# Row normalization by the sum of absolute values: moving a sixth of the scaling from ScalarE to VectorE

## The chip, the cores and the metric

The kernel runs on one core of one Trainium2 chip. The metric is device time in microseconds (us). The span of a profile is about 2 us shorter than the device time of the same run. Most executions agree within 0.3%.

The engines that matter are VectorE (DVE in the profile), ScalarE (ACT), the sequencer SP, which issues the loads, and the 16 DMA engines, which move everything between HBM (the main memory) and SBUF (the on-chip memory).

## The reference

```python
def setup_inputs():
    batch, seq, dim = 32, 512, 1024
    return {"x": np.random.randn(batch, seq, dim).astype(np.float32)}

def reference(x):
    sums = np.sum(np.abs(x), axis=-1, keepdims=True)
    return (x / (sums + 1e-8)).astype(np.float32)
```

These are 16384 rows of 1024 fp32 numbers: 67.1 MB are read and 67.1 MB written. Nothing is reused.

## The kernel before

Each of the 128 partitions gets 128 rows, 12 at a time: ten tiles of 12 rows per partition and a last one of 8. A tile is loaded, reduced, scaled in place and stored. There are four tile buffers, so up to four tiles are under way at once.

```python
    R = 12
    BUFS = 4
    # ... (piece() picks rows; pools: sbuf with BUFS buffers, stats with 4)

    def normalize(x_tile, r0, k, kv):
        s = stats.tile([P, R], FP32)
        nc.vector.tensor_reduce(out=s[:, :k], in_=x_tile[:, r0 : r0 + k, :],
            axis=mybir.AxisListType.X, op=mybir.AluOpType.add,
            apply_absolute_value=True)
        # ... add EPS to s, inv = reciprocal of s, both on VectorE
        nc.vector.tensor_mul(                       # VectorE: rows 0 .. kv-1
            out=x_tile[:, r0 : r0 + kv, :], in0=x_tile[:, r0 : r0 + kv, :],
            in1=inv[:, :kv].unsqueeze(2).to_broadcast([P, kv, d]))
        for r in range(kv, k):                      # ScalarE: rows kv .. k-1
            row = x_tile[:, r0 + r, :]
            nc.scalar.activation(out=row, in_=row,
                func=mybir.ActivationFunctionType.Copy, scale=inv[:, r : r + 1])

    with tc.manual_schedule():
        for i, k in enumerate(rows):
            x_tile = sbuf.tile([P, R, d], FP32)
            nc.sync.dma_start(out=x_tile[:, :k, :], in_=piece(x_flat, i))
            normalize(x_tile, 0, k, k // 2)
            nc.scalar.dma_start(out=piece(out_flat, i), in_=x_tile[:, :k, :])
```

A store waits for both halves of the scaling. A load waits until the store of the tile four places earlier has landed, because it needs that tile's buffer.

## Time and profile before

The median was 317.85 us (three runs, 317.69 to 318.0); the profiled run has a span of 315.8 us.

| | before |
|---|---|
| VectorE busy | 212.4 us (67%) |
| ScalarE busy | 69.0 us (22%) |
| 16 DMA engines: time of all packets | 98.9% of the span |
| traffic over the span | 425 GB/s |

From the page of the kernel before: the busy time of each engine; the DMA row of the 40 slices (tenths of busy time); the two DMA queues, q1 for loads and q10 for stores, with packets, MB and the share of 16 engines' span that the packets took.

```profile
DVE 212.4 (67%) x44; ACT 69.0 (22%) x65; POOL 0.2 (0%) x4
...
DMA  8999999999999999999999999999999999999996
...
q1 hardware_dynamic: 1584, 67.11, 49.8%
q10 hardware_dynamic: 1584, 67.11, 49.1%
```

Add the two queues: 98.9% of 315.8 us is 312.3 us in which each of the 16 engines, on average, was moving a packet. So at most 3.5 us can be gained without making the traffic itself cheaper.

The window table of the same kernel agrees. Its columns are the stretch, its length, the busy time of each engine with its instructions, the clock, the DMA share, and GB/s. A share a little over 1 comes from packets being put into windows whole.

```profile
60.00:290.00 230.00, 166.06 (x33) 50.75 (x48) 0.00 (x0) 1.00 1.00 434
290.00:300.00 10.00, 4.92 (x4) 4.27 (x4) 0.00 (x0) 1.00 1.02 442
300.00:316.00 16.00, 0.00 (x0) 0.00 (x0) 0.00 (x0) 1.00 0.78 336
```

The groups by form give the price of each operation: line, engine, operation, output and input shape, count, then total busy us and mean ns, then idle time before.

```profile
L45 DVE TENSOR_REDUCE s<-x_tile 128x12 f32<-128x12288 f32 x10 | 129.5, 12952 | 76.9 <-DMA x_tile<-in_x_dram 76.9
L62 ACT ACTIVATE x_tile<-x_tile,inv 128x1024 f32<-128x1024 f32 x64 | 67.7, 1135 | 207.6 <-DVE inv L54 207.6
L55 DVE TENSOR_TENSOR x_tile<-x_tile,inv 128x6144 f32<-128x6144 f32 x10 | 65.6, 6557 | 0.3
...
L55 DVE TENSOR_TENSOR x_tile<-x_tile,inv 128x4096 f32<-128x4096 f32 x1 | 4.4, 4425 | 0.0
```

The table of waits (who waited for whom, total us, times, longest) shows both compute engines waiting for data:

```profile
ACT x_tile L62 <- DVE inv L54: 207.6, 11, 22.7
DVE s L45 <- DMA x_tile<-in_x_dram: 81.1, 9, 18.4
```

The chain of work that ended last, by engine, from the page:

```profile
DMA 55%; DVE 25%; another core or an unknown queue 9%; ACT 4%; issue 0%; SPq 0%; DVEq 0%; ACTq 0%
```

The end of the timeline (start us, length, what it was; ACTq is ScalarE's queue, which issues the stores). The last store is issued at 295.18:

```profile
277.40 0.34 ACTq L74 DMA_DIRECT2D out_dram<-x_tile  x1
281.44 8.69 DVE L45 TENSOR_REDUCE s<-x_tile 128x8 f32<-128x8192 f32 x1 [4.13 <-DMA x_tile<-in_x_dram]
...
290.67 4.42 DVE L55 TENSOR_TENSOR x_tile<-x_tile,inv 128x4096 f32<-128x4096 f32 x1
295.18 0.34 ACTq L74 DMA_DIRECT2D out_dram<-x_tile  x1
```

By the landing records of the trace (the times at which the DMA engines report a transfer done), the store issued at 277.40 landed only at 305.05, so the last store found the DMA engines still busy with the one before.

### The profile page before, as it was taken

What the parts mean: (1) busy time and instruction counts of PE and PEld (TensorE: products, weight loads), DVE (VectorE), ACT (ScalarE), POOL (GpSimd) and SP (SyncE); (2) the same over time, 40 slices, a digit from 0 to 9 for tenths busy, and PEclk for the clock granted to TensorE, in tenths of its full rate; (3) what the DMA queues carried; (4) which work ended last, traced back from release to release, by engine and by line L of the source; (5) the groups of instructions that cost most, each with busy time, mean ns of one, the idle gap of its engine ahead of it and who ended that gap; (6) DMA issues with size and microseconds to landing.
All of it is one profiled execution on the core that took longest, in us unless ns stands there. A gap on an engine that the chain in (4) does not pass through costs nothing.

```text
span 315.8 us, 227 instructions
## 1 busy us (share of the span) xinstructions
DVE 212.4 (67%) x44; ACT 69.0 (22%) x65; POOL 0.2 (0%) x4
## 2 busy tenths in 40 slices
DVE  0069999998499079719944991797099449949300
ACT  0010804308007000700440070007003400701300
POOL 0000000000000000000000000000000000000000
DMA  8999999999999999999999999999999999999996
GB/s 311 467 417 411 467 367 442 405 454 430 417 448 430 423 461 423 436 442 417 442 442 411 449 436 411 448 436 423 448 430 436 442 413 450 421 448 417 448 403 278
DMA packets 3169, 134.23 MB, mean 425 GB/s; under 512 B 352, under 2 KB 352, under 8 KB 352
## 3 DMA queue, kind: packets, MB, share of 16 engines
q1 hardware_dynamic: 1584, 67.11, 49.8%
q10 hardware_dynamic: 1584, 67.11, 49.1%
q14 instruction: 1, 0.01, 0.0%
HBM read 67.11 MB, written 67.11 MB: 425 GB/s over the span
## 4 chain that ended last, share of the span: by engine, by line
DMA 55%; DVE 25%; another core or an unknown queue 9%; ACT 4%; issue 0%; SPq 0%; DVEq 0%; ACTq 0%
DMA x_tile<-in_x_dram 41%; DVE s L45 19%; DMA out_dram<-x_tile 14%; DVE x_tile L55 6%; ACT x_tile L62 4%; DVE inv L54 0%; DVE s L52 0%; SPq L72 0%; DVEq L54 0%; ACTq L74 0%
## 5 line engine op out<-in xcount | busy, mean ns | idle before, releaser
L45 DVE TENSOR_REDUCE s<-x_tile 128x12 f32<-128x12288 f32 (+1 forms) x11 | 138.2, 12564 | 81.1 <-DMA x_tile<-in_x_dram 81.1
L62 ACT ACTIVATE x_tile<-x_tile,inv 128x1024 f32<-128x1024 f32 x64 | 67.7, 1135 | 207.6 <-DVE inv L54 207.6
L55 DVE TENSOR_TENSOR x_tile<-x_tile,inv 128x6144 f32<-128x6144 f32 (+1 forms) x11 | 70.0, 6364 | 0.4
L62 ACT ACT_TABLE_LOAD x1 | 1.3, 1283 | 18.4 <-DMA x_tile<-in_x_dram 18.4
L54 DVE RECIPROCAL inv<-s 128x12 f32<-128x12 f32 (+1 forms) x11 | 2.5, 226 | 0.9
L52 DVE TENSOR_SCALAR s<-s 128x12 f32<-128x12 f32 (+1 forms) x11 | 1.9, 173 | 0.4
L89 POOL MEMSET const-bfloat16-1.0<- 128x1 bf16 x1 | 0.1, 101 | 0.0
L89 POOL MEMSET const-uint8-127<- 128x1 uint8 x1 | 0.1, 101 | 0.0
L89 POOL MEMSET const-float32-0.0<- 128x1 f32 x1 | 0.1, 98 | 0.2 <-issue 0.2
L89 POOL MEMSET const-float32-1.0<- 128x1 f32 x1 | 0.1, 98 | 0.0
## 6 DMA issues: line engine op xcount, KB each, us to landing
x_tile<-in_x_dram SPq DMA_DIRECT2D x10, 6144.0 KB, 38.5
out_dram<-x_tile ACTq DMA_DIRECT2D x10, 6144.0 KB, 53.5
x_tile<-in_x_dram SPq DMA_DIRECT2D x1, 4096.0 KB, 33.7
out_dram<-x_tile ACTq DMA_DIRECT2D x1, 4096.0 KB, 19.5
```

The costliest lines, as they stand in the source:

```text
L45: nc.vector.tensor_reduce(out=s[:, :k], in_=x_tile[:, r0 : r0 + k, :], axis=mybir.AxisListType.X, op=mybir.AluOpType.add, apply_absolute_v ...
L52: nc.vector.tensor_scalar_add(out=s[:, :k], in0=s[:, :k], scalar1=EPS)
L54: nc.vector.reciprocal(out=inv[:, :k], in_=s[:, :k])
L55: nc.vector.tensor_mul(out=x_tile[:, r0 : r0 + kv, :], in0=x_tile[:, r0 : r0 + kv, :], in1=inv[:, :kv].unsqueeze(2).to_broadcast([P, kv, d]),)
L62: nc.scalar.activation(out=row, in_=row, func=mybir.ActivationFunctionType.Copy, scale=inv[:, r : r + 1],)
L89: nc = _bacc.Bacc("TRN2", target_bir_lowering=False, num_devices=1)
```

## The change

The intent is to shift work between the two compute engines. VectorE scales 8 of 12 rows (6 of the last 8) in place of half, and ScalarE scales the others. The number of instructions on VectorE stays the same; ScalarE has 22 fewer.

```diff
-            normalize(x_tile, 0, k, k // 2)
+            normalize(x_tile, 0, k, k - k // 3)
```

## The prediction

> **What bounds the kernel now.** The DMA engines. The row of tenths shows DMA at 9 in all but the first and last of 40 slices; the window table gives a DMA share of 0.99 to 1.00 and 430 to 435 GB/s from 60 to 290 us. In the trace's packets all 16 engines carry one from 1.7 to about 312 us without a gap: a 48 KB packet takes 1815 ns, and 160 such plus 16 of 32 KB per engine make about 310 us (estimate: 160 x 1.815 + 16 x 1.21). The rest of the 315.8 us span is the start and an uneven finish. The Trainium skill, "DMA: Bandwidth & Descriptors", Specifications, gives 435 GB/s as the fabric ceiling; the trace agrees. VectorE is busy 67%, ScalarE 22%. In the table of waits VectorE waited 81.1 us for loads, about 8.9 per later tile.
>
> The chain of waits puts 25% of the span on VectorE. That misleads: meanwhile other tiles' transfers keep the 16 engines full.
>
> **What the change does.** The same bytes move; 22 fewer ScalarE rows (64 to 42). Per tile VectorE scales 8 rows in place of 6 (last tile 6 for 4), ScalarE 4 in place of 6 (last 2 for 4). In the trace VectorE takes 4.42 us for 4 rows and 6.56 for 6: two rows cost 2.14 us, 8 rows about 8.70. "VectorE: DVE Perf Modes" of the Trainium skill, section on the TRN2 errata, gives (N+151)/0.96 ns for an fp32 tensor_tensor: 6.56 us for N=6144, which the trace confirms, and 8.69 for 8192. ScalarE needs 6.34 us for 6 rows, about 4.2 for 4. The two ran side by side and ended within 0.2 us of each other; now VectorE ends last and each store is issued about 2.14 us later.
>
> VectorE busy goes from 212.4 to about 236 us (75%), ScalarE from 69.0 to about 46 (14%). VectorE's work per tile rises from 20.0 to 22.1 us, under the 29.0 us in which a tile's 12.6 MB pass through DMA.
>
> **The critical path.** Delaying every store matters only if the DMA engines run dry. With four buffers, a tile spends 20 of its 116 us (4 x 29) in compute, the rest in queued or moving transfers; with 22 the queues stay about three tiles deep. Start: the first four loads alone keep DMA busy to about 58 us; the first store moves from 38.5 to 40.6. VectorE's first four tiles then follow each other without idling (the fourth reduction at about 85 us, before 83.3), with loads and stores still queued. End: the last store is issued at 295.2, while the previous one lands only at 305.0: about 10 us of slack against 2.14. Added time on the critical path: about 0.
>
> **Predicted: 317.9 us, range 317.2 to 318.8** (before: 317.69 to 318.0). Faster by over 2%: 0.01; within 2%: 0.97; slower by over 2%: 0.02.
>
> **What would show it.** Right: span near 315.8, DMA 9 throughout, packets still 1815 ns; VectorE's multiply 8.70 us; its wait for loads down to about 60 us (about 6.8 per tile); the last store issued about 297 with the earlier one still moving. Wrong: a slice of low DMA in the middle or at 295 to 300; packets longer than 1815 ns; a multiply slower than 8.7 us.
>
> **What would make it wrong.** Load and store queues both empty for a moment because the delay shifts their phase; a last store that comes after the store queue is dry; a more uneven finish of the 16 engines, worth about 1 us; packets that slow because loads and stores mix differently.

## The result, and the profile after

| | before | after |
|---|---|---|
| time, median of 6 runs | 317.77 us | 317.24 us |
| range | 317.46 to 318.05 | 317.03 to 317.67 |
| span of the profiled run | 315.8 us | 315.7 us |
| VectorE busy | 212.4 us | 235.8 us |
| ScalarE busy | 69.0 us | 46.1 us |
| packets, per DMA engine | 312.3 us | 311.9 us (98.8% of 315.7) |

The ratio is 0.9984, with a 95% interval from 0.9971 to 0.9997. A ratio here is always the mean time of one kernel's fast runs over the mean of the other's in the same rounds, so it is not quite the ratio of the medians. By the 2% criterion the two are the same.

The page of the changed kernel, same lines as before:

```profile
DVE 235.8 (75%) x44; ACT 46.1 (15%) x43; POOL 0.2 (0%) x4
...
DMA  8999999999999999999999999999999999999996
...
q1 hardware_dynamic: 1584, 67.11, 49.7%
q10 hardware_dynamic: 1584, 67.11, 49.1%
```

VectorE gained 23.4 us and ScalarE lost 22.9, and the DMA rows are those of before. The window table:

```profile
60.00:290.00 230.00, 189.19 (x37) 35.25 (x34) 0.00 (x0) 1.00 1.00 434
290.00:300.00 10.00, 5.44 (x1) 1.07 (x2) 0.00 (x0) 1.00 1.04 452
300.00:316.00 16.00, 0.00 (x0) 0.00 (x0) 0.00 (x0) 1.00 0.76 327
```

In the middle stretch VectorE worked 23 us more, and DMA still moved 434 GB/s. The groups by form show what a multiply of 8 rows costs, and that the wait for loads gave way by as much as the work grew:

```profile
L45 DVE TENSOR_REDUCE s<-x_tile 128x12 f32<-128x12288 f32 x10 | 129.5, 12950 | 55.9 <-DMA x_tile<-in_x_dram 55.9
L55 DVE TENSOR_TENSOR x_tile<-x_tile,inv 128x8192 f32<-128x8192 f32 x10 | 86.9, 8692 | 0.3
L62 ACT ACTIVATE x_tile<-x_tile,inv 128x1024 f32<-128x1024 f32 x42 | 44.9, 1137 | 226.3 <-DVE inv L54 226.3
```

The table of waits:

```profile
DVE s L45 <- DMA x_tile<-in_x_dram: 58.0, 8, 18.6
```

81.1 us of waiting became 58.0: 23.1 us less wait for 23.4 us more work. That is what it looks like when added work lands in slack.

The timelines show how. Here is the sixth tile in both kernels, its reduction and the issue of its store, first before and then after:

```profile
141.21 12.95 DVE L45 TENSOR_REDUCE s<-x_tile 128x12 f32<-128x12288 f32 x1 [8.93 <-DMA x_tile<-in_x_dram]
161.38 0.34 ACTq L74 DMA_DIRECT2D out_dram<-x_tile  x1
139.07 12.95 DVE L45 TENSOR_REDUCE s<-x_tile 128x12 f32<-128x12288 f32 x1 [6.76 <-DMA x_tile<-in_x_dram]
161.37 0.34 ACTq L74 DMA_DIRECT2D out_dram<-x_tile  x1
```

The load landed about 2.1 us earlier and the store was issued at the same time. The same holds from the fifth tile to the eighth, with store issues within 0.1 us of those before; the last three were 0.2 to 0.35 us later. Only the first four stores were clearly late, by 2.4, 4.5, 6.7 and 3.7 us.

The chain that ended last:

```profile
another core or an unknown queue 36%; DMA 31%; DVE 26%; SPq 0%; issue 0%; DVEq 0%; ACTq 0%
```

Its DMA and unknown parts changed a great deal with no change in time. That is a warning against reading a gain off these shares. ScalarE has left the chain, because it now ends before VectorE. The end of the timeline:

```profile
277.61 0.34 ACTq L74 DMA_DIRECT2D out_dram<-x_tile  x1
279.65 8.69 DVE L45 TENSOR_REDUCE s<-x_tile 128x8 f32<-128x8192 f32 x1 [2.13 <-DMA x_tile<-in_x_dram]
```

The last store was issued at 295.53 (the issue record), and the store before it landed at 305.00. The last landing was at 314.67, against 314.72 before.

### The profile page after: what moved, and what is told of

Same layout as the page of the kernel before. It is cut to its first block, busy times and chain, and to the rows that moved or that the text cites. A ratio compares the mean times of both kernels' runs of the same rounds, so it can differ in the third digit from the quotient of the medians.

```text
span 315.7 us, 205 instructions
## 1 busy us (share of the span) xinstructions
DVE 235.8 (75%) x44; ACT 46.1 (15%) x43; POOL 0.2 (0%) x4
## 4 chain that ended last, share of the span: by engine, by line
another core or an unknown queue 36%; DMA 31%; DVE 26%; SPq 0%; issue 0%; DVEq 0%; ACTq 0%
DMA x_tile<-in_x_dram 15%; DMA out_dram<-x_tile 15%; DVE s L45 15%; DVE x_tile L55 10%; SPq L72 0%; DVE inv L54 0%; DVE s L52 0%; DVEq L54 0%; ACTq L74 0%
## 5 line engine op out<-in xcount | busy, mean ns | idle before, releaser
L55 DVE TENSOR_TENSOR x_tile<-x_tile,inv 128x8192 f32<-128x8192 f32 (+1 forms) x11 | 93.5, 8498 | 0.4
L62 ACT ACTIVATE x_tile<-x_tile,inv 128x1024 f32<-128x1024 f32 x42 | 44.9, 1137 | 226.3 <-DVE inv L54 226.3
```

What stands on the lines that cost most here:

```text
L55: nc.vector.tensor_mul(out=x_tile[:, r0 : r0 + kv, :], in0=x_tile[:, r0 : r0 + kv, :], in1=inv[:, :kv].unsqueeze(2).to_broadcast([P, kv, d]),)
L62: nc.scalar.activation(out=row, in_=row, func=mybir.ActivationFunctionType.Copy, scale=inv[:, r : r + 1],)
```

## The experiments

Theory A is that of the prediction: the 16 DMA engines pass the same packets without a gap, and the split of the computation is hidden. The rivals are these. B: the share of the chain on VectorE is real time. C: the 0.5 us is a real gain that comes with fewer ScalarE rows. D: the shift of rows is free in itself, whatever the buffers. E: the end of the last tile is exposed. Two more, F and G, came later.

### 1. How little does the computation matter?

Four kernels ran on the same chip with five rounds each; the fourth is that of experiment 2. First, the changed kernel again.

> The changed kernel once more, in five rounds, to size the 0.5 us by which it was ahead. Theory A (all of the time is the 16 DMA engines passing the same packets, the split between VectorE and ScalarE is hidden): same, ratio to before 0.997 to 1.002. Rival C (a real small gain comes with fewer ScalarE rows): 0.9984 again with an interval that stays below 1.

It took 317.25 us against 317.44 of before; ratio 0.9994, interval 0.9982 to 1.0005. The interval of the first comparison did not reach 1, this one does. The gain of 0.5 us is not confirmed.

Second, no computation at all:

```diff
-            normalize(x_tile, 0, k, k - k // 3)
```

> No computation at all, each tile is loaded and stored again (wrong result on purpose): what the DMA traffic alone costs. Theory A: same, within 1% of before, 315.5 to 318; a packet of 48 KB still takes 1815 ns. Rival B: clearly faster, 10% or more, as the chain has 26% of its time on VectorE and ScalarE.

It took 317.32 us; ratio to before 0.9995 (0.9983 to 1.0007). The result was wrong. Its page has the DMA row of the kernel before, digit for digit, and these queues:

```profile
q1 hardware_dynamic: 1584, 67.11, 49.8%
q10 hardware_dynamic: 1584, 67.11, 49.1%
```

That is 98.9% of its span of 315.5 us, or 312.0 us of packets per engine. Loading and storing alone takes as long as the whole kernel. This is the strongest evidence for theory A, and it refutes rival B for the kernel before: VectorE and ScalarE had 29% of its chain, and taking away all they do gains nothing that can be measured.

Third, the opposite of the change, with ScalarE scaling 8 of 12 rows:

```diff
-            normalize(x_tile, 0, k, k - k // 3)
+            normalize(x_tile, 0, k, k // 3)
```

> The opposite of the change: ScalarE 8 rows of 12, VectorE 4. VectorE falls to about 17.8 us per tile, ScalarE's part is 8.5 us, the store is issued about 1.9 us later than in the kernel before. Theory A: same, 317 to 318.5. Rival B: faster by several us, since VectorE has less. Rival C: slower than before, about 318.3, ratio above 1.

It took 317.06 us, ratio 0.9988 (0.9975 to 1.0001), with VectorE busy for 188.9 us and ScalarE for 91.8. Rival B and rival C both fall. B wanted several us; C wanted a loss where the median is even a little lower than before.

### 2. All rows on VectorE: theory A missed

```diff
-            normalize(x_tile, 0, k, k - k // 3)
+            normalize(x_tile, 0, k, k)
```

> All rows scaled by VectorE, none by ScalarE: VectorE needs about 26.4 us per tile (12.95 reduction, 0.4, about 13.0 multiply) of the 29.0 us that DMA needs, and each store is issued about 6.5 us later than in the kernel before. Theory A: same, 316.5 to 319 us, VectorE about 90% busy. Rival B (the share of the chain of waits that lies on VectorE is real time, so more VectorE work costs): at 6.4 us more per tile over 11 tiles, up to 60 us slower, at least several us. Rival C: faster again than the changed kernel, about 316.5.

It took 325.93 us (322.99 to 327.31); ratio 1.0261 (1.0227 to 1.0295). This was not expected by theory A, though VectorE needs 26.3 us per tile, which is less than DMA's 29.0. It is far from rival B's 60 us too, although 8.5 us does meet B's "at least several us": this run alone would not refute B, the copy does. The queues on its page:

```profile
q1 hardware_dynamic: 1584, 67.11, 48.4%
q10 hardware_dynamic: 1584, 67.11, 47.8%
```

96.2% of its span of 325.2 us is 312.8 us: the packets took only 0.9 us more per engine than in the changed kernel. The loss is idle time, 12.4 us per engine against 3.8. The window table (this kernel has no ScalarE column) shows where:

```profile
60.00:290.00 230.00, 221.30 (x34) 0.00 (x0) 1.00 0.99 428
290.00:300.00 10.00, 9.90 (x5) 0.00 (x0) 1.00 0.93 398
300.00:310.00 10.00, 7.84 (x1) 0.00 (x0) 1.00 0.76 328
310.00:326.00 16.00, 0.00 (x0) 0.00 (x0) 1.00 0.51 217
```

The holes are at the end. By the packet records (those of 8 KB and more) the engines idled only about 0.15 us each from 5 to 285 us (0.10 in the changed kernel), and about 11 us after that (2.4). The last load landed at 289.24 in place of 279.63, and VectorE needed 17.8 us for that tile, so the last store was issued only at 307.87. The landing records tell more. A transfer is spread over 16 engines, and the records give the first and the last of the 16 to land. For stores:

| | changed kernel | all rows on VectorE |
|---|---|---|
| store 1 | 72.72 to 75.08 | 75.89 to 80.33 |
| store 2 | 101.69 to 104.12 | 97.61 to 107.76 |
| store 6 | 217.69 to 220.12 | 212.06 to 226.93 |
| last store | 313.34 to 314.67 | 318.81 to 324.28 |

In store 6 fifteen of the 16 had landed by 215.65 us, and the last at 226.93. From about 75 us on, one straggler was behind the others in every transfer. The records do not name the engine, so that it is the same one each time is an inference from its steady lag. A load into a freed buffer waits for the last of the 16 engines, so it was issued late (at 226.97 after that store), and in the end VectorE got its last tiles late. In the last store the straggler was 5.5 us behind the first; for the last 5 us of packets, from 318.7 to 323.95, it worked alone.

The packet records show where the lag began. From 56.95 to 74.38 us eight 48 KB packets, stores and loads in turn, follow each other end to start, so they are most likely those of one engine. Six of them took 1.88 to 2.69 us in place of 1.815, and the eight took 2.9 us more than usual together. No other 48 KB packet that began between 51 and 83 us took over 1.83 us. In store 1 the last engine landed 3.7 us after the one before it. So the lag began with slower packets on one engine; why they were slower was not tested.

### 3. Where does the hiding end? Theory F

The loads gave a hint. From the issue of the fifth load to the landing of the fourth there were 9.6 us before (issued at 73.67, landed at 83.24) and 5.9 in the changed kernel (75.15, 81.06). With all rows on VectorE it was -0.2 (80.41, 80.17): the load queue ran dry, although the engines still had stores to move and did not idle there. Theory F says that a later store is free until then. Rival G says that the loss grows in step with VectorE's share. Ten of 12 rows on VectorE lie between:

```diff
-            normalize(x_tile, 0, k, k - k // 3)
+            normalize(x_tile, 0, k, k - k // 6)
```

> VectorE scales 10 of 12 rows (7 of the last 8), ScalarE 2 (1): VectorE about 24.2 us per tile, each store issued about 4.3 us later than in the kernel before. Theory F (the delay is free until the queue of loads runs dry: from the issue of the fifth load to the landing of the fourth there were 9.6 us in the kernel before, 5.9 in the changed one, and -0.2 with all rows on VectorE, about 1.7 us less per us of store delay, my estimate from these): an overlap of about 2.2 us is left, so the time stays within 0.5% of before, 316.8 to 318.8. Rival G (the loss grows in step with VectorE's share beyond the changed kernel, half of the 8.5 us that all rows on VectorE cost): about 321.5, ratio about 1.013.

It took 322.05 us (321.99 to 322.19, four runs); ratio 1.0147 (1.0125 to 1.017). Theory F falls. (By the 2% criterion this is still "same", but the interval is clear of 1, and the time lies outside F's 0.5%.) The overlap was -0.3 us (issued at 81.43, landed at 81.17), not the 2.2 that I had extrapolated. Rival G has the right number, but its two points are not one mechanism, as the page shows:

```profile
q1 hardware_dynamic: 1584, 67.11, 49.8%
q10 hardware_dynamic: 1584, 67.11, 48.8%
```

98.6% of 320.4 us is 315.9 us. Here the engines had almost no more idle time (4.5 us against 3.8), but their packets took 4.0 us more per engine, of the 4.7 us by which the span grew. The window table says the same, with a full DMA share at a lower rate:

```profile
60.00:290.00 230.00, 204.56 (x34) 17.50 (x16) 0.00 (x0) 1.00 1.00 428
```

By the packet records, nearly all the longer packets beyond those of the changed kernel fell between 52 and 124 us. In that stretch 141 of 604 packets of 48 KB took over 1.9 us in place of 1.815, most of them 2.0 to 2.5; in the changed kernel none did. A burst of longer packets as the first store begins is nothing special: between 40 and 52 us 17 took over 2.0 us in the kernel before, 27 in the changed one and 20 here. What is special here is that it did not stop. From 124 us on they took 1.815 again, although VectorE's work per tile was the same. The slow packets began well before the load queue ran dry at 81 us, so the dry queue did not cause them. What set them off is open. The straggler of experiment 2 began in the same stretch and with longer packets too, but on one engine; whether the two have one cause is open as well. The ten-row split ran on another chip than experiments 1 and 2, but the kernel before took 317.66 us there, so that chip was not slower as such.

### 4. The end of the last tile

The prediction counted on about 10 us of slack at the end. An extra VectorE reduction, before the multiply of the last tile alone, delays the last store by a known amount. The first kernel reduces 6 rows once, the second reduces 8 rows twice.

```diff
+        if k < R:
+            waste = stats.tile([P, R], FP32)
+            for _ in range(1):                  # second kernel: range(2)
+                nc.vector.tensor_reduce(
+                    out=waste[:, :6],           # second kernel: :8
+                    in_=x_tile[:, r0 : r0 + 6, :],  # second kernel: + 8
+                    # ... axis, op and absolute value as above
+                )
         nc.vector.tensor_mul(
```

> The changed kernel with an extra VectorE reduction of 6 rows (about 6.5 us, result unused) before the multiply of the last tile alone, so the last store is issued at about 302 in place of 295.5, while the store before it lands at about 305. Theory A (about 10 us of slack at the end): 0 to 1 us slower. Rival E (the end of the last tile is exposed): 6.5 us slower.

It took 317.92 us; ratio 1.0016 (0.9996 to 1.0035). The last store was issued at 302.42. Its windows show no hole:

```profile
300.00:305.00 5.00, 2.33 (x1) 0.00 (x0) 0.00 (x0) 1.00 0.95 410
305.00:310.00 5.00, 0.00 (x0) 0.00 (x0) 0.00 (x0) 1.00 1.00 433
```

> The same with two extra reductions of 8 rows (about 17.4 us), so the last store is issued at about 313, after the one before it has landed. Theory A: slower by 17.4 less the slack of about 8 to 10 us, that is 7.5 to 10 us, and the DMA row shows a hole before the last store. Rival E: 17.4 us slower.

It took 327.22 us; ratio 1.0302 (1.0289 to 1.0316), 9.6 us over the 317.60 of before in these rounds. The last store was issued at 312.68, and the hole is in plain sight:

```profile
300.00:305.00 5.00, 5.00 (x1) 0.00 (x0) 0.00 (x0) 1.00 0.68 295
305.00:310.00 5.00, 4.96 (x2) 2.19 (x2) 0.00 (x0) 1.00 0.00 0
310.00:326.00 16.00, 2.59 (x1) 0.00 (x0) 0.00 (x0) 1.00 0.61 263
```

Of 17.4 us, about 8 were hidden. A delay of 6.5 us was hidden nearly whole. Rival E falls; the slack of the prediction was somewhat large, but of the right size.

### 5. VectorE above DMA's pace

A second, unused reduction in every tile (the edit of experiment 4 with `if True` and all k rows) takes VectorE past 29.0 us per tile.

> The changed kernel with a second, unused reduction in every tile, so VectorE needs about 35.1 us per tile, more than the 29.0 us of DMA. Theory A: now VectorE bounds it: 18.4 us first load + 10 x 35.1 + 24.4 for the small tile + about 12 for its store = 406 us (398 to 412), VectorE over 90% busy, holes in the DMA row. Rival B (VectorE was on the path already): 12.95 us per tile on top of 317 us, 10 x 12.95 + 8.7 = 138 us more, about 455 us.

It took 405.79 us, where theory A said 406; ratio 1.2776. In its table of waits VectorE waits for the first load and never again:

```profile
DVE s L45 <- DMA x_tile<-in_x_dram: 18.4, 1, 18.4
```

So this is what a VectorE bound looks like in this kernel. In the changed kernel VectorE still waited in 8 of 11 tiles.

### 6. Fewer buffers: what the change costs when nothing hides it

```diff
-    BUFS = 4
+    BUFS = 1        # and 2; each with the split of before and of the change
```

> The kernel before with one tile buffer in place of four, so that load, computation and store of a tile follow each other: reference for the next run. About 17 us load, 20 us computation, 17 us store for each of 10 tiles and about 37 us for the small one: 560 to 600 us.

> The changed kernel with one buffer. Theory A: with nothing in the queues to hide it, the later store costs its full 2.14 us in each of 11 tiles, 23.5 us more than the half split with one buffer (22 to 25 us), about 4%. Rival D (the shift of rows is free in itself, buffers do not matter): within 3 us of the half split.

With one buffer the half split took 579.74 us and the changed split 602.48. The changed split costs 22.7 us, against the 23.5 us by which 11 tiles of 2.14 us would delay it. In the timelines one round, from one 12-row reduction's start to the next, takes 53.89 us with the half split (72.05 to 125.94) and 56.10 with the other (74.61 to 130.71). Rival D falls. The change does have a price, and the buffers pay it.

> The kernel before with two buffers. Two tiles' traffic takes 58 us, one buffer's round about 54 us when it waits for nothing, so gaps in DMA are likely but small: 320 to 360 us, and gaps in the DMA row.

> The changed kernel with two buffers. Theory A: part of the 2.14 us per tile shows, between 0 and 12 us (half of 11 tiles' 2.14 us, as two tiles go round together) over the half split with two buffers. Rival D: within 2 us.

With two buffers it was 366.03 us and 366.98 us (364.42 to 368.61). The half split was slower than I had expected (320 to 360), so the DMA engines lost more than I thought. The difference of 0.95 us lies within the scatter of the second kernel, so this pair does not tell theory A from rival D.

## Why the prediction was right

The predicted time was 317.9 us with a range of 317.2 to 318.8; measured were 317.24, and 317.25 in the repeat. That is within the range, near its lower edge.

- **What bounds the kernel.** Shown. The copy without any computation takes 317.32 us.
- **What the change moves.** Predicted VectorE busy about 236 us, measured 235.8; ScalarE about 46, measured 46.1. The multiply of 8 rows was to take 8.70 us and took 8.692. The Trainium skill, "VectorE: DVE Perf Modes", section on the TRN2 errata, gives (N+151)/0.96 ns, which is 8.69 us; here it holds up to N = 12288 as well (12.96 us measured with all rows on VectorE, 12.96 by the formula).
- **The wait for loads** was to fall from 81 to about 60 us, 6.8 per later tile. It fell to 58.0, with 6.8 in most later tiles.
- **The start.** The first store was to be issued at 40.6 us and was at 40.86. The fourth reduction was to start at about 85 us without idling and started at 84.81.
- **The end.** The last store was to be issued at about 297 us and was at 295.53, because the last load landed 1.8 us earlier than before (279.63 against 281.42). This is one case of what the prediction had wrong on its way to the right time: "each store is issued about 2.14 us later". VectorE set the pace of the first four tiles, so there the delay added up, to 6.7 us in the third store; from the fifth tile on it was nearly gone, because the loads landed 1.8 to 2.2 us earlier. This fits with the loads having had the DMA engines to themselves longer at the start: the first packet of a store began at 45.0 us in place of 43.3. About 9.5 us were left until the landing of the store before. Experiment 4 shows that a delay of 6.5 us there is still nearly free and one of 17.4 is not.
- **What was too simple.** The prediction argued that VectorE's 22.1 us are "under the 29.0 us in which a tile's 12.6 MB pass through DMA". That was enough for this change, but it is no safe criterion, and to that extent the prediction had luck: the same sentence would have passed the splits with 10 and 12 rows. At 24.2 us per tile the time was 1.5% longer, and at 26.3 us it was 2.6% longer. "Delaying every store matters only if the DMA engines run dry" was too simple as well: the ten-row split lost 4.4 us with engines that were nearly always busy. The prediction also named the chance of "packets that slow because loads and stores mix differently". The trace of the ten-row split does show slower packets, though not their cause; in the changed kernel they ended with the burst before 52 us, which the kernel before has too.

The Trainium skill, "SBUF — State Buffer", section "SBUF: two separate sides", says that a DMA cannot be slowed by a compute op. In the kernels of before and after and in the copy this agrees: 312.3, 311.9 and 312.0 us of packets per engine. In the ten-row split the packets took 315.9 us; no run here shows whether the computation caused that or only the timing of the stores.

## What to carry to other kernels

Add up the time of all packets over the 16 engines first. If it fills the span, as it did here with 98.9%, moving work between compute engines cannot help, whatever the chain of waits gives to them. Then check that it does not hurt either: look at how long before the earlier store's landing the last one is issued, at how far apart the 16 engines land, and at how long the packets take. How long the load queue stays filled at the start did not foretell the loss here (theory F). A compute engine below DMA's pace per tile is not by itself safe: here losses showed from 24.2 of 29.0 us on. A copy without computation is the cheapest way to learn the floor.

## What the Trainium skill lacked or had wrong

- "DMA: Bandwidth & Descriptors" has no figure for how far the 16 engines can drift apart within one large transfer. Here the first and the last engine of a 6 MB store landed 2.4 us apart in the changed kernel, and up to 14.9 us apart with all rows on VectorE, where one engine stayed behind and delayed every buffer.
- The same page gives the fabric ceiling of 435 GB/s, with which the trace agrees (434), though no run here shows that it is the fabric that binds. It does not say that packets of the same size can take longer while all engines stay busy: 48 KB packets took 1.815 us in steady state and 141 of 604 of them over 1.9 us, most 2.0 to 2.5, between 52 and 124 us of the ten-row split.
- "Perfetto Trace Analysis", section "Identifying the Most-Contended Engine", points to HBM utilization for DMA in place of occupancy. Here the share of packet time summed over the 16 engines (98.9%) told more, since it separates idle engines (96.2% with all rows on VectorE) from slow packets (98.6% of a longer span with ten rows).
